# One two-bank PSUM tile and one maximum for the two score maps of a differential attention head

## The chip, the cores and the metric

The kernel runs on one core of a Trainium2 chip. The metric is the device time of one execution in microseconds (us). A core has a matrix engine (TensorE, PE in the profile), a vector engine (VectorE, DVE), a scalar engine (ScalarE, ACT), GpSimd (POOL) and SyncE (SP), whose queue issues nearly all of the DMA transfers here. Each engine works through its own instructions in the order of the program and waits for the others by semaphores.

## What is computed

One inference step of a two-layer transformer over 128 context tokens and 256 latent tokens, in fp32. Layer 0 mixes by retention and by windowed attention, layer 1 by differential attention and a Fourier transform, and a SwiGLU block follows each. The change concerns the differential attention of layer 1, cut from the reference:

```python
dq = dq.reshape(B, T, H_DIFF, 2, HEAD_DIM)        # 6 heads, 2 maps each, 64 wide
dk = dk.reshape(B, T, H_DIFF, 2, HEAD_DIM)
...
s = jnp.einsum('bqhmd,bkhmd->bhmqk', qb, keys).astype(f32) * (HEAD_DIM ** -0.5)
p = jax.nn.softmax(s, axis=-1)
p = p[:, :, 0] - lam_full * p[:, :, 1]
return jnp.einsum('bhqk,bkhe->bqhe', p.astype(vals.dtype), vals)
```

Every head has two softmax maps, and the second, times a factor, is subtracted from the first before the values are applied.

## The kernel before

The 384 tokens are three blocks of 128 rows: block 0 is the context, blocks 1 and 2 are the latent. A block of context has 128 keys, a latent block 384 (256 latent, 128 cached). So there are 18 items (block, head), and each has two score maps of 128 x 128 or 128 x 384.

`mixer_cd` computes layer 1's mixer. It projects the tokens with five slabs of 512 weight columns (`in_block`, line 377, tiles `cd`; three fp32r matmuls per product, from a weight split into a rounded part `r_` and a rest `l_` by ScalarE and VectorE, lines 173 and 175), transposes queries and keys into `dqT` and `dkT`, and calls `scores(upto)` three times between the slabs, for two heads each time. `scores` takes the items in the order of the list `items` and keeps `sc1` up to two items ahead of `sc2`.

`sc1(b, h)` computes the two maps of an item. Map m has its 64 features on partitions 64m to 64m+63 of `dqT` and `dkT`, so the two matmuls (lines 1216 and 118, tiles `ds`) use different rows of the array. Each matmul of fp32 is two records in the trace. Each map has a one-bank PSUM tile of its own out of four (`Banks("pcd", S=4)`, line 1154). VectorE takes the maximum of each map (line 1217, tile `dnm`), scales both by -0.125 (line 1219), and ScalarE forms the exponentials with their row sums (line 1223, tiles `dp` and `dsum`).

`sc2(b, h)` inverts the sums (line 1232), scales the second map (1233), adds it to the first (1234), and TensorE transposes the result in blocks of 128 x 128 (tiles `td`), which ScalarE copies (line 386). Between them TensorE has the projections `cd`, transpositions `tcd` of queries and keys, and the two Fourier steps `y` and `z`.

The order of the instructions on each engine is not written out. A scheduler lays them out when the program is built: work issued under `boost` (lines 116 to 121; among it the score matmuls, through `hmm`, and the transpositions) goes ahead of other work as soon as the scheduler holds it ready, and the projections fill in. On the chip each engine then keeps that fixed order.

The windowed attention of layer 0 (`win1`) also has two maps for each of its items and puts them in one tile of two banks (`bk.pair`, tiles `ws`), with one maximum (line 872, tile `wnm`).

Of the kernel before, what the change touches and what calls it, by code (L numbers as in the profile page):

```python
# [14 lines left out]
AF = mybir.ActivationFunctionType  # L15
ALU = mybir.AluOpType
AX = mybir.AxisListType
PSUM = bass.MemoryType.PSUM

P = 128  # L20
# [44 lines left out]
def trunk_kernel(ctx: ExitStack, tc: tile.TileContext, a: dict):  # L65
    nc = tc.nc
    mm = nc.tensor.matmul
    V, S, G, SY = nc.vector, nc.scalar, nc.gpsimd, nc.sync
# [4 lines left out]
    def opened(name, **kw):  # L73
        st = ExitStack()
        return st.enter_context(pool(name, **kw)), st
# [6 lines left out]
    def bankA(name):  # L82
        return psA.tile([P, 512], F32, tag="A", name=name)
# [19 lines left out]
    def small(shape, name):  # L103
        tick[0] += 1
        n = 1
        for s in shape[1:]:
            n *= s
        return perm.tile(shape, F32, tag=f"sm{n}", name=f"{name}{tick[0]}", bufs=SMALL[n])
# [4 lines left out]
    def mid(shape, name):  # L113
        return perm.tile(shape, F32, tag="uf", name=name, bufs=3)

    def boost(f, *args, **kw):
        with tc.high_priority(offset=BOOST):
            return f(*args, **kw)  # L118

    def hmm(*args, **kw):  # L120
        return boost(mm, *args, **kw)
# [1028 lines left out]
    def mixer_cd(u, cat, pto, u1, t1):  # L1150
        o_k = a["o_diff_k"][0, 0].rearrange("t h m d -> t (h m d)")
        o_v = a["o_diff_v"][0, 0].rearrange("t h d -> t (h d)")
        slab = cd_slab
        bk = Banks("pcd", S=4)
        ap, ap_es = opened("attn_cd")
        rope_of[0] = ap.tile([P, 2, 2, 64], F32, name="rope1")
        S.dma_start(rope_of[0], a["k_rope"].rearrange("b p s d -> p b s d"))
        if True:
            nlam, sub = lamd["nlam"], lamd["sub"]
            dqT = ap.tile([P, H_DIFF, NTOK], F32, name="dqT")  # L1160
            dkT = ap.tile([P, H_DIFF, 512], F32, name="dkT")
# [4 lines left out]
            for i, n in ((0, 4), (4, 2)):  # L1166
                t = mid([P, 512], f"ck{i}")
# [38 lines left out]
            def sc1(b, h):  # L1206
                nk = 1 if b == 0 else 3
                k0 = 0 if b == 0 else P
                w = nk * P
                nm = small([P, 2], "dnm")  # L1210
                sums = small([P, 2], "dsum")
                pss = []
                for m in range(2):
                    rows = slice(64 * m, 64 * m + 64)
                    ps = bk("S", f"ds{b}_{h}_{m}")
                    hmm(ps[:, 0:w], dqT[rows, h, b * P : (b + 1) * P], dkT[rows, h, k0 : k0 + w], start=True, stop=True)
                    V.reduce_max(nm[:, m : m + 1], ps[:, 0:w], AX.X)
                    pss.append(ps)
                V.tensor_scalar(nm, nm, -0.125, None, ALU.mult)
                pm = []  # L1220
                for m in range(2):
                    t = ap.tile([P, 384], F32, tag="p", name=f"dp{b}_{h}_{m}", bufs=5)
                    S.activation(t[:, 0:w], pss[m][:, 0:w], AF.Exp, bias=nm[:, m : m + 1], scale=0.125,
                                 accum_out=sums[:, m : m + 1])
                    pm.append(t)
                st_of[b, h] = (pm, sums)
# [18 lines left out]
            def scores(upto):  # L1245
                while state["n2"] < upto:
                    while state["n1"] < min(state["n2"] + 2, len(items)) and (state["n1"] < upto or upto == len(items)):
                        sc1(*items[state["n1"]])
                        state["n1"] += 1
                    sc2(*items[state["n2"]])  # L1250
                    state["n2"] += 1
# [59 lines left out]
            for b in range(NB):  # L1311
                ps = bankA(f"cd4_{b}")
# [6 lines left out]
            for b in range(NB):  # L1319
                ps = bankA(f"cd3_{b}")  # L1320
# [23 lines left out]
    m = {}  # L1344
    xscr = dram.tile([NB, P, D], F32, tag="xscr", name="xscr")
    for l in range(2):
# [9 lines left out]
        if l == 0:  # L1356
            def mod_ab(v, bk):
                mp = mod_pe(0, v, bk("M", f"mod0_{v}"))
                if v == 2:
                    m[0, v] = mod_scratch(mp, f"0_{v}")  # L1360
                else:
                    m[0, v] = mod_cols(mp, 0, v, bk("M", f"modt0_{v}"))

            pre, wxr_es = mixer_ab(u, cat, early, early_es, ap1, ap1_es, pto, *first, [lambda bk, v=v: mod_ab(v, bk) for v in (2, 3, 4)])
        else:
            cat, cat_es = open_cat(1)
            mixer_cd(u, cat, pto, m["s1"], m["t1"])
            pre, wxr_es = [], None
# [154 lines left out]
```

## Time and profile before

| | us |
|---|---|
| three timed runs | 1017.32, 1020.04, 1021.83 |
| their median | 1020.04 |
| the profiled execution | 1018.55 |
| its span, first to last instruction | 1016.8 |
| TensorE busy in it | 996.9 |
| VectorE busy | 637.9 |
| ScalarE busy | 432.9 |

The span is what the trace covers; the execution's own time is 1.75 us more. Busy time counts a matmul from its start to its modelled end, and matmuls are pipelined: a projection row lasts 0.40 us and the next one starts 0.23 us after it. Rows of one kind that follow each other directly are merged, with their count behind an x. What a matmul costs is therefore read from the start of one row to the start of the next. Time in brackets at the end of a row is idle time of the engine ahead of it, with what ended it.

### The profile page before, as it was taken

To read this page: it belongs to the slowest core of one execution; us is meant where nothing else is said; L and a number is where in the kernel's file an instruction comes from. 1 tells how busy PE (TensorE), PEld (TensorE's weight loads), DVE (VectorE), ACT (ScalarE), POOL (GpSimd) and SP (SyncE) were. 2 spreads that over 40 slices of the span, in tenths; PEclk is the share of its full clock that TensorE was granted. 3 is DMA by queue.
4 is the path that set the end of the run, shared out by engine and by line. 5 is a ranking of instruction groups with operands and counts; after the bars stand their busy time and mean duration, and the time that the engine had idled before them with its cause. 6 is when DMAs were issued, how large, how long until landed. Compare 5 with 4: busy or idle time off the path is not lost.

```text
span 1016.8 us, 14891 instructions
## 1 busy us (share of the span) xinstructions
PE 996.9 (98%) x5679; PEld 829.7 (82%) x5679; DVE 637.9 (63%) x1356; ACT 432.9 (43%) x786; POOL 1.2 (0%) x5
## 2 busy tenths in 40 slices
PE   9999999999999999999999999999999999999996
PEld 4775567688898988989987766787889999999985
DVE  5477558588785977968567677558843333335554
ACT  3385533227543333333428555544833333333410
POOL 0000000000000000000000000000000000000000
PEclk9999999999999999999999999999999999999998
DMA  9975446472896767676615322235574444444401
GB/s 305 294 203 187 146 132 205 171 254 94 281 301 219 217 211 253 208 235 208 207 63 161 95 88 93 83 103 224 184 252 146 125 125 124 125 125 127 161 22 41
DMA packets 109703, 172.85 MB, mean 170 GB/s; under 512 B 10176, under 2 KB 78272, under 8 KB 109632
## 3 DMA queue, kind: packets, MB, share of 16 engines
q1 hardware_dynamic: 106960, 170.87, 52.8%
q10 hardware_dynamic: 2672, 1.04, 0.4%
q8 instruction: 44, 0.72, 0.3%
q14 instruction: 27, 0.22, 0.1%
HBM read 167.52 MB, written 4.36 MB: 169 GB/s over the span
## 4 chain that ended last, share of the span: by engine, by line
PE 91%; DMA 3%; DVE 3%; ACT 2%; issue 1%; ACTq 0%; DVEq 0%
PE dn L518 17%; PE wu L542 17%; PE wg L542 17%; PE cd L377 8%; PE wo L377 6%; PE rvg L377 3%; PE s L377 3%; PE rqk L377 2%; DMA rawm<-in_w_mod 2%; PE ds L118 2%; PE hg L377 2%; PE mod L118 1%; PE hu L377 1%; PE ms L118 1%; PE po L118 1%; PE wpo L118 1%
## 5 line engine op out<-in xcount | busy, mean ns | idle before, releaser
L542 PE MATMUL wg<-ulf,r_wg 128*128 128x384 f32 x320 | 108.4, 339 | 0.0
L542 PE MATMUL wu<-ulf,r_wu 128*128 128x384 f32 x320 | 108.3, 338 | 0.0
L542 PE MATMUL wu<-urf,r_wu 128*128 128x384 f32 x320 | 108.2, 339 | 0.0
L542 PE MATMUL wg<-urf,l_wg 128*128 128x384 f32 x320 | 108.1, 338 | 0.0
L542 PE MATMUL wu<-urf,l_wu 128*128 128x384 f32 x320 | 108.1, 338 | 0.0
L542 PE MATMUL wg<-urf,r_wg 128*128 128x384 f32 x320 | 108.0, 339 | 0.0
L175 DVE TENSOR_TENSOR l_wg<-raw_wg,r_wg 128x1024 fp32r<-128x1024 f32 x40 | 48.7, 1223 | 68.4 <-ACT r_wg L173 68.4
L249 DVE SCALAR_TENSOR_TENSOR z<-mraw,cs,z 128x1024 f32<-128x1024 f32 x70 | 86.3, 1280 | 8.3 <-DMA mraw<-in_w_mod 8.0
L175 DVE TENSOR_TENSOR l_wd<-raw_wd,r_wd 128x1024 fp32r<-128x1024 f32 x36 | 44.0, 1223 | 53.7 <-ACT r_wd L173 53.7
L173 ACT CAST r_wd<-raw_wd 128x1024 fp32r<-128x1024 f32 x36 | 37.8, 1050 | 87.0 <-PE wu L542 40.1
L175 DVE TENSOR_TENSOR l_wu<-raw_wu,r_wu 128x1024 fp32r<-128x1024 f32 x40 | 48.6, 1222 | 40.1 <-ACT r_wu L173 40.1
L173 ACT CAST r_wg<-raw_wg 128x1024 fp32r<-128x1024 f32 x40 | 42.0, 1050 | 73.0 <-PE dn L518 29.9
L173 ACT CAST r_wu<-raw_wu 128x1024 fp32r<-128x1024 f32 x40 | 42.0, 1049 | 64.6 <-issue 24.2
L518 PE MATMUL dn<-l_wd,hr 128*128 128x512 f32 x168 | 66.6, 396 | 0.0
L518 PE MATMUL dn<-r_wd,hr 128*128 128x512 f32 x168 | 66.5, 396 | 0.0
L518 PE MATMUL dn<-r_wd,hl 128*128 128x512 f32 x168 | 66.5, 396 | 0.0
L542 PEld LDWEIGHTS wg<-urf,r_wg 128*128 128x128 f32 x320 | 60.1, 188 | 1.9 <-issue 0.8
L542 PEld LDWEIGHTS wu<-urf,r_wu 128*128 128x128 f32 x320 | 60.1, 188 | 1.7 <-ACT r_wg L173 0.8
L542 PEld LDWEIGHTS wu<-ulf,r_wu 128*128 128x128 f32 x320 | 60.1, 188 | 0.5
L542 PEld LDWEIGHTS wg<-ulf,r_wg 128*128 128x128 f32 x320 | 60.1, 188 | 0.5
L542 PEld LDWEIGHTS wg<-urf,l_wg 128*128 128x128 f32 x320 | 60.1, 188 | 0.0
L542 PEld LDWEIGHTS wu<-urf,l_wu 128*128 128x128 f32 x320 | 60.1, 188 | 0.0
(418 smaller groups left out, 2180.0 us busy)
## 6 DMA issues: line engine op xcount, KB each, us to landing
raw_wd<-in_w_down SPq DMA_DIRECT2D x44, 512.0 KB
rawm<-in_w_mod SPq DMA_DIRECT2D x40, 512.0 KB
mraw<-in_w_mod SPq DMA_DIRECT2D x40, 512.0 KB
raw_wg<-in_w_gate SPq DMA_DIRECT2D x40, 512.0 KB
raw_wu<-in_w_up SPq DMA_DIRECT2D x40, 512.0 KB
raw_cd<-in_w_in_cd SPq DMA_DIRECT2D x20, 512.0 KB
ms<-in_w_mod SPq DMA_DIRECT2D x16, 512.0 KB
raw_rqk<-in_w_in_ab SPq DMA_DIRECT2D x16, 256.0 KB
```

What stands on the lines that cost most here:

```text
L118: return f(*args, **kw)
L173: S.copy(r, t)
L175: V.tensor_tensor(lo, t, r, ALU.subtract)
L249: V.scalar_tensor_tensor(z[c], t, cs[:, c, k : k + 1], z[c], ALU.mult, ALU.add)
L377: op = mm(ps[:, col : col + width], u[pu][:, k0 + kk, b * P : (b + 1) * P], (r, lo)[pw][:, kk, :], start=(first and i == 0 and pu + pw == ...
L518: mm(acc[b, nh], h[fc][ph][:, b * P : (b + 1) * P], wrl[pw][:, nh * 512 : (nh + 1) * 512], start=(fc == 0 and ph + pw == 0), stop=(last an ...
L542: mm(ps[j][:, 0:NTOK], un[i][pw][:, k, j * P : (j + 1) * P], u2[pu][:, 4 * i + k, :], start=(i == 0 and k == 0 and pu + pw == 0), stop=(i ...
```

## The change

The two maps of an item share one tile of two banks: `bk.pair` gives a tile of 2 x 512 columns, of which there are two (S=2, the same four banks). Map m is written to bank m of it. One `reduce_max` over both banks writes both maxima, after the loop instead of in it. Scale, exponentials and everything behind them are as before.

```diff
-        bk = Banks("pcd", S=4)
+        bk = Banks("pcd", S=2)
...
-                pss = []
+                ps = bk.pair("S", f"ds{b}_{h}")
                 for m in range(2):
                     rows = slice(64 * m, 64 * m + 64)
-                    ps = bk("S", f"ds{b}_{h}_{m}")
-                    hmm(ps[:, 0:w], dqT[rows, h, b * P : (b + 1) * P], dkT[rows, h, k0 : k0 + w], start=True, stop=True)
-                    V.reduce_max(nm[:, m : m + 1], ps[:, 0:w], AX.X)
-                    pss.append(ps)
+                    hmm(ps[:, m, 0:w], dqT[rows, h, b * P : (b + 1) * P], dkT[rows, h, k0 : k0 + w], start=True, stop=True)
+                V.reduce_max(nm, ps[:, :, 0:w], AX.X)
                 V.tensor_scalar(nm, nm, -0.125, None, ALU.mult)
...
-                    S.activation(t[:, 0:w], pss[m][:, 0:w], AF.Exp, bias=nm[:, m : m + 1], scale=0.125,
+                    S.activation(t[:, 0:w], ps[:, m, 0:w], AF.Exp, bias=nm[:, m : m + 1], scale=0.125,
```

Two lines fewer in the file move the lines behind: the maximum is line 1216 in the new file, its scaling 1217, the reciprocal 1230, the scaling of the second map 1231, the subtraction 1232.

Since the scheduler lays out the order from the instructions and their tiles, it is another one around the scores. On TensorE, in head 1, the old order has, from the first map of block 1 on (ds1_1_0 is block 1, head 1, map 0; the last number of a name is only a counter):

```order
L118 MATMUL ds1_1_0_5932<-dkT_5470,dqT_5469 128x384
L118 MATMUL ds1_1_1_5935<-dkT_5470,dqT_5469 128x384
L118 MATMUL tcd2_0_5810<-ident_69,t1cd2_0_5776 128x128 x4
L118 MATMUL ds2_1_0_5952<-dkT_5470,dqT_5469 128x384
L118 MATMUL td2_0_5925<-ident_69,dp2_0_0_5895 128x128 x3
L118 MATMUL ds2_1_1_5955<-dkT_5470,dqT_5469 128x384
L377 MATMUL cd2_1_5779<-r_cd2_0_5590,ul1_5057 128x512
L118 MATMUL td0_1_5947<-ident_69,dp0_1_0_5917 128x128
L377 MATMUL cd2_1_5779<-l_cd2_0_5591,ur1_5056 128x512
L118 MATMUL ds0_2_0_6094<-dkT_5470,dqT_5469 128x128
```

and the new one, from the transposition tcd2_0 on:

```order
L118 MATMUL tcd2_0_5810<-ident_69,t1cd2_0_5776 128x128 x4
L377 MATMUL cd2_1_5779<-l_cd2_0_5591,ur1_5056 128x512
L118 MATMUL ds1_1_5924<-dkT_5470,dqT_5469 128x384 x2
L118 MATMUL td2_0_5917<-ident_69,dp2_0_0_5889 128x128 x3
L118 MATMUL ds2_1_5942<-dkT_5470,dqT_5469 128x384 x2
L118 MATMUL td0_1_5937<-ident_69,dp0_1_0_5909 128x128
L377 MATMUL cd2_1_5779<-r_cd2_1_5596,ur1_5056 128x512
L377 MATMUL cd2_1_5779<-r_cd2_1_5596,ul1_5057 128x512
L377 MATMUL cd2_1_5779<-l_cd2_1_5597,ur1_5056 128x512
L377 MATMUL cd2_1_5779<-r_cd2_1_5596,ur1_5056 128x512
L118 MATMUL ds0_2_6082<-dkT_5470,dqT_5469 128x128 x2
```

Both maps of an item stand together in the new order (x2), and what stood between them stands before or behind. On TensorE in head 3, the old order reads, from block 1 on:

```order
L118 MATMUL ds1_3_0_6171<-dkT_5470,dqT_5469 128x384
L118 MATMUL td1_2_6142<-ident_69,dp1_2_0_6114 128x128 x3
L118 MATMUL ds1_3_1_6174<-dkT_5470,dqT_5469 128x384
L118 MATMUL ds2_3_0_6191<-dkT_5470,dqT_5469 128x384
L118 MATMUL td2_2_6164<-ident_69,dp2_2_0_6134 128x128 x3
L118 MATMUL ds2_3_1_6194<-dkT_5470,dqT_5469 128x384
L118 MATMUL z0_0_6438<-y0_0_6433,cpe_6300 128x128
L118 MATMUL td0_3_6186<-ident_69,dp0_3_0_6156 128x128
```

and the new one:

```order
L118 MATMUL ds1_3_6151<-dkT_5470,dqT_5469 128x384 x2
L118 MATMUL td2_2_6144<-ident_69,dp2_2_0_6116 128x128 x3
L118 MATMUL ds2_3_6169<-dkT_5470,dqT_5469 128x384 x2
L118 MATMUL td0_3_6164<-ident_69,dp0_3_0_6136 128x128
L118 MATMUL z0_0_6402<-y0_0_6397,cpe_6276 128x128 x2
```

The transposition td0_3 now stands right behind the pair ds2_3, ahead of the Fourier step z. On VectorE at the same place the old order is:

```order
L1217 TENSOR_REDUCE dnm144_6169<-ds1_3_1_6174 128x1
L1232 RECIPROCAL dsum143_6148<-dsum143_6148 128x2
L1219 TENSOR_SCALAR dnm144_6169<-dnm144_6169 128x2
L1233 TENSOR_SCALAR dp0_3_1_6158<-dp0_3_1_6158,dsum143_6148,nlam_759 128x128
L1234 SCALAR_TENSOR_TENSOR dp0_3_0_6156<-dp0_3_0_6156,dsum143_6148,dp0_3_1_6158 128x128
L1217 TENSOR_REDUCE dnm146_6189<-ds2_3_0_6191 128x1
```

and the new one:

```order
L1232 SCALAR_TENSOR_TENSOR dp2_2_0_6116<-dp2_2_0_6116,dsum141_6110,dp2_2_1_6118 128x384
L1230 RECIPROCAL dsum143_6130<-dsum143_6130 128x2
L1231 TENSOR_SCALAR dp0_3_1_6138<-dp0_3_1_6138,dsum143_6130,nlam_759 128x128
L1216 TENSOR_REDUCE dnm144_6149<-ds1_3_6151 128x2
L1232 SCALAR_TENSOR_TENSOR dp0_3_0_6136<-dp0_3_0_6136,dsum143_6130,dp0_3_1_6138 128x128
```

The joint maximum of ds1_3 stands between the scaling of dp0_3_1 and the subtraction into dp0_3_0, which td0_3 reads. On ScalarE only neighbouring instructions change places around the scores; the queue of SyncE with the DMA issues and GpSimd are as before.

## Rows read from the trace of the kernel before

**Rows 1.** The page, busy time, share of the span, instructions: TensorE

```profile
PE 996.9 (98%) x5679; PEld 829.7 (82%) x5679; DVE 637.9 (63%) x1356; ACT 432.9 (43%) x786; POOL 1.2 (0%) x5
```

**Rows 2.** Busy time by windows (from:to, length, engines, clock, DMA share, GB/s)

```profile
591.02:605.70 14.68, 14.58 (x65) 8.72 (x64) 9.60 (x31) 8.84 (x29) 0.00 (x0) 1.00 0.15 52
617.51:646.90 29.39, 28.45 (x127) 16.70 (x126) 21.98 (x68) 19.26 (x65) 0.00 (x0) 1.00 0.06 22
```

**Rows 3.** Waits of the DMA queue, 560 to 720: total, times, longest

```profile
SPq L164 <- DVE l_cd L175: 78.4, 15, 32.3
```

**Rows 4.** Timeline of TensorE, windowed attention, one item: start, duration, instruction

```profile
104.19 0.92 PE L118 MATMUL ws<-wkT,wqT 64*128 64x384 f32 x4
105.04 0.28 PE L118 MATMUL ws<-wmb,identb 128*128 128x128 bf16 x2
```

**Rows 5.** Timeline of TensorE, heads 1 and 2 of the differential attention

```profile
594.41 1.47 PE L118 MATMUL ds<-dkT,dqT 64*128 64x384 f32 x4
595.81 0.66 PE L118 MATMUL tcd<-ident,t1cd 128*128 128x128 f32 x4
...
597.71 0.91 PE L118 MATMUL ds<-dkT,dqT 64*128 64x384 f32 x2
598.55 0.50 PE L377 MATMUL cd<-r_cd,ul 128*128 128x512 f32 x1
...
600.08 0.39 PE L377 MATMUL cd<-r_cd,ul 128*128 128x512 f32 x1
600.39 0.48 PE L118 MATMUL ds<-dkT,dqT 64*128 64x128 f32 x2
600.81 0.50 PE L377 MATMUL cd<-l_cd,ur 128*128 128x512 f32 x1
601.14 0.39 PE L377 MATMUL cd<-r_cd,ur 128*128 128x512 f32 x1
601.37 0.40 PE L377 MATMUL cd<-r_cd,ul 128*128 128x512 f32 x1
```

**Rows 6.** Timeline of TensorE, heads 3 to 5

```profile
620.77 0.49 PE L118 MATMUL ds<-dkT,dqT 64*128 64x128 f32 x2 [0.70 <-ACT dp L1223]
...
634.84 0.30 PE L118 MATMUL td<-ident,dp 128*128 128x128 f32 x1 [0.16 <-DVE dp L1234]
...
636.83 0.91 PE L118 MATMUL ds<-dkT,dqT 64*128 64x384 f32 x2
637.67 0.55 PE L118 MATMUL td<-ident,dp 128*128 128x128 f32 x3
638.15 1.91 PE L118 MATMUL ds<-dkT,dqT 64*128 64x384 f32 x6
639.99 0.55 PE L118 MATMUL td<-ident,dp 128*128 128x128 f32 x3
```

**Rows 7.** Instructions by tile, ds and ws: shortest/median/longest ns, first and last start, forms

```profile
L1217 DVE TENSOR_REDUCE dnm<-ds x36: 279/549/558, 575.0 to 640.8; 128x1 f32<-128x384 f32 x24, 128x1 f32<-128x128 f32 x12
L1223 ACT ACTIVATE dp<-ds,dnm x36: 357/580/609, 575.7 to 642.3; 128x384 f32<-128x384 f32 x24, 128x128 f32<-128x128 f32 x12
...
L872 DVE TENSOR_REDUCE wnm<-ws x12: 412/954/958, 66.3 to 129.2; 128x2 f32<-128x768 f32 x8, 128x2 f32<-128x256 f32 x4
```

**Rows 8.** Timeline of VectorE, heads 2 to 4

```profile
619.84 0.17 DVE L1219 TENSOR_SCALAR dnm<-dnm 128x2 f32<-128x2 f32 x1
619.92 1.02 DVE L1217 TENSOR_REDUCE dnm<-ds 128x1 f32<-128x384 f32 x2
...
626.46 0.35 DVE L1234 SCALAR_TENSOR_TENSOR dp<-dp,dsum,dp 128x128 f32<-128x128 f32 x1
...
634.35 0.34 DVE L1234 SCALAR_TENSOR_TENSOR dp<-dp,dsum,dp 128x128 f32<-128x128 f32 x1
```

## The prediction

> **What bounds the kernel now.** The page comes first. TensorE is busy for 996.9 of 1016.8 us [rows 1], but its matmuls are pipelined and a busy row may hide a wait, so the starts of successive rows have to be read, not the busy share. The change touches the scores of the differential attention alone. In the order of TensorE's instructions the two programs differ in two stretches: 591.02 to 605.70 us (heads 0 to 2) and 617.51 to 646.90 us (heads 2 to 5). The view by windows gives both [rows 2]: TensorE is busy 14.58 of 14.68 and 28.45 of 29.39 us, VectorE only 9.60 and 21.98, the clock is granted in full (1.00, the upper level), and DMA moves little (0.15 and 0.06 of its share). So TensorE's own queue sets the pace here. What is saved on TensorE in these 44 us should come off the end: behind them the weight loads wait for buffers that VectorE's splits free (78.4 us in 15 waits [rows 3]), these splits wait for matmuls, and so loads start earlier with TensorE.
>
> **What is removed: maps that ran alone.** The two maps of a head use rows 0 to 63 and 64 to 127 of the array. The windowed attention at the start already has its two maps in one two-bank tile, which is the nearest row for the new form. Side by side, its two maps (four records) start at 104.19, and the next instruction starts at 105.04: 0.85 us for both [rows 4]. One map alone, two records, costs as much: 597.71 to 598.55, 0.84 us [rows 5]. Two maps next to each other overlap; two with something between them cost double.
>
> I counted, in the old order, the maps that have something else between them. Of 384 columns: in heads 1 and 4 one pair stands apart. In heads 3 and 5 two pairs do, but the second map of one stands beside the first of the next, so three slots serve where two would. In head 5: 0.84 from 636.83 to 637.67, then 1.84 from 638.15 to 639.99 [rows 6], which is 0.85 + 0.84 with a wait of 0.15. That is one slot of 0.84 us too many in each of four heads: **3.4 us**. Of 128 columns: in heads 2 to 5 block 0's maps stand apart. A map alone between full matmuls costs 600.08 to 600.39, to 600.81, to 601.14 [rows 5], that is 0.31 + 0.42 + 0.33 less two full matmuls of 0.23 (601.14 to 601.37): 0.60 us. Three heads save this; in head 5 the second map stands among other short work and saves its 0.42. Together **2.2 us**. In the new order both maps of every pair are adjacent, so all of it goes.
>
> Old waits go too. The pair at 594.41 takes 1.40 us to 595.81 instead of 0.85, since its second map waits for a bank: 0.55 us [rows 5]. Before 620.77 TensorE is idle for 0.70, for an exponential; before 634.84 for 0.16 [rows 6]; with the 0.15 of head 5 that is 1.0 us. **Removed: 3.4 + 2.2 + 0.55 + 1.0 = 7.15 us of TensorE's time.**
>
> **What is shortened beside TensorE.** 36 maxima become 18. Two separate ones of 384 columns take 2 x 549 ns, and the joint one of 768 takes 954 ns in the windowed attention [rows 7]: 144 ns saved, twelve times. Two of 128 columns take 2 x 279, joint 412: 146 ns, six times. The sum, 2.6 us of VectorE, I cost at nothing by itself: VectorE idles 7.4 us of the second stretch [rows 2]. It acts only where TensorE waits for VectorE, and there it is in the walk below. The exponentials stay 36.
>
> **What is added: new waits.** Two of them. First, a slot is now two banks: a pair waits until *both* exponentials of the pair two before are done, where its first map waited for the first alone; one exponential of 384 columns is 580 ns [rows 7]. Behind the waiting pair stand the whole of TensorE's in-order queue, the long projections among it. Second, on VectorE the joint maximum cannot start before both maps are done, and the scheduler has put it ahead of work that TensorE needs. In head 3 the old order ran the subtraction of dp0_3 right behind its scaling; in the new order the maximum of ds1_3 stands between them, and the transposition td0_3 waits for that subtraction.
>
> I walked the new order through with the rows' durations, each instruction as early as its engine's queue, its row's duration and what it waits for allow. At this place, from the start of pair ds1_3: its end is at 0.92 [rows 4]; behind it the three transpositions of td2_2 (0.48, as 637.67 to 638.15 [rows 6]) and the pair ds2_3 let td0_3 come up at 2.27. On VectorE the subtraction of dp2_2, the reciprocal and the scaling are done at 1.50. The maximum then takes 0.95 [rows 7] and the subtraction 0.35 (626.46 [rows 8]). It starts some 0.08 before the maximum ends, as the maximum at 619.92 starts 0.09 before the scaling of 619.84 ends [rows 8]: 2.72. From VectorE to TensorE it is another 0.15 (634.35 + 0.34 [rows 8], then 634.84 [rows 6]): 2.87: a wait of 0.60 us. The other waits over 0.2 us in this walk are td0_1 0.33, the pair ds0_3 0.32 (second exponential), td2_3 0.27, td0_4 0.46, td0_5 0.33 and td1_5 0.21. **Added: 2.5 us.** Smaller gaps stand in both orders and are left out on both sides. No row shows these waits, so both ends: nothing, if the maxima come earlier than I have them; at most all of what is removed and more, if each of the twelve pairs in the tight parts waits as long as the worst wait shown, 0.70: 8.4 us. I take 2.5, which is nearest to what the old order has in the same places (1.0 + 0.55).
>
> VectorE's load in the second stretch is 21.98 us of 29.39 [rows 2]; TensorE's part would shrink to about 24 without new waits, so VectorE fits, but with little room. On this the Trainium skill warns ("TensorEngine Tiling (Array Packing)", Performance Considerations, PSUM Bottleneck): tiling makes TensorE faster but not the emptying of PSUM, which may become the bottleneck. By that rule the gain would stop where VectorE is full; by the row it isn't full yet, and the rule's case is the second rival below.
>
> **The sum.** 7.15 - 2.5 = 4.65 us less. The profiled execution took 1018.55 us (span 1016.8 and 1.75 around it); 4.65 less is 1013.9. The median of the three timed runs is 1020.04, which would give 1015.4. The median of all four times shown is 1019.3, and from it I forecast **1014.7 us**. About 0.5% (5.1 us) is what a measurement of this kernel can tell from no change, so the forecast lies just inside of it.
>
> **Rivals.** *The new waits don't come.* Then 7.15 us go: 1012.2. For it: VectorE idles in both stretches, and the joint maximum is shorter. Against it: the subtraction stands behind the maximum in a fixed order. *VectorE's chain becomes the bound.* Each of twelve pairs in the tight parts waits some 0.4 us for maximum, subtraction and transposition, the middle of what the walk found: 4.8 us given back, 2.35 gained, 1016.9. For it: VectorE is busy three quarters of the second stretch already. Against it: only seven places in the walk waited as long as 0.2. *The slots bind, slower than before.* With two slots of two banks every pair waits one exponential longer than a first map did: 12 x 0.58 = 7.0 us, on top of the 2.5: 9.5 given back against 7.15, 1021.6. It decides from 0.6 us a pair. The Trainium skill points that way ("Perfetto Trace Analysis", Optimizing Tensor Performance, Matmuls): independent groups should rotate through different banks, so that emptying one overlaps the next group's matmuls. No row of the new form shows such a wait, and between pairs the new order has transpositions and projections, which cover most of it. *That the change does not do what it says* can be left out: in the new order the two matmuls of each pair stand together, and the windowed attention shows that two maps in one tile overlap [rows 4].
>
> **Chances.** Forecast (3.2 to 6.0 us gained) 0.60; no new waits (over 6.0) 0.16; VectorE's chain (0 to 3.2) 0.19; slots (slower) 0.05. Of the forecast's 0.60 some 0.22 lies over 5.1 us, so faster by over 0.5% 0.22 + 0.16 = 0.38, within 0.5% 0.38 + 0.19 = 0.57, slower 0.05. Low end: all of 7.15 and 0.7 for the spread of the runs, 1011.5. High end: 1 us gained, 1018.3, which leaves out the slower case and a part of the third.
>
> **What would show it.** In the profile of after: every pair's four records in one row of 0.85 us, and no two-record rows; these two stretches shorter by 2 and 3 us; the wait of td0_3 for the subtraction at about 0.6 us, those of score pairs for exponentials at 0.3 or less; 18 maxima at 954 and 412 ns; and all behind it shifted by the same amount. The forecast is wrong if TensorE's idle time before score pairs passes 3 us, if a pair stays at 1.7 us, or if the weight loads behind don't move with TensorE.

## The result

| | us, median (lowest to highest) |
|---|---|
| before, 4 runs | 1019.37 (1017.32 to 1021.83) |
| after, 4 runs | 1012.06 (1011.55 to 1012.68) |
| ratio | 0.9929, 95% interval 0.9909 to 0.9948 |
| profiled execution, before and after | 1018.55 and 1011.62 |
| its span, before and after | 1016.8 and 1009.8 |

The changed kernel is faster by 0.7%, more than the 0.5% that can be told from no change. 1014.7 had been forecast, and the time lies in the range, at its lower part. A second measurement of the same kernel gave less, 0.56% (first experiment below). Of the kernel of e4 and e8 one execution each is left out, at 1043.12 and 1042.73 us (mean granted clock 0.979, 0.995 or more in all others); that of e4 was its profiled one, with the clock at its lower level from 635.9 to 670.0 us, so the kernel ran once more for a profile (e8).

**Where the time went.** Every profile has a row by which the program can be cut into three: the first score row (tile `ds`), the row of 36 matmuls `dpv` at the end of the attention, and the end. Timeline of TensorE after (start, duration, instruction, count; idle time before it in brackets):

```profile
572.96 0.49 PE L118 MATMUL ds<-dkT,dqT 64*128 64x128 f32 x4
...
667.90 4.19 PE L118 MATMUL dpv<-dv,dpT 128*128 128x128 f32 x36
```

In the profile of before the same rows start at 574.49 and 674.47. So, in us:

| | before | after | difference |
|---|---|---|---|
| start to the first score row | 574.49 | 572.96 | -1.53 |
| first score row to the `dpv` row | 99.98 | 94.94 | -5.04 |
| `dpv` row to the end | 342.28 | 341.92 | -0.36 |

The middle part holds all that the change touches. The two stretches in which the orders differ, by windows (from:to, length, then busy time of PE, PEld, DVE, ACT and POOL with their instructions, granted clock, DMA share, GB/s), each from the same instruction to the same as in [rows 2]:

```profile
589.52:602.41 12.89, 12.47 (x66) 7.66 (x64) 9.05 (x26) 8.58 (x28) 0.00 (x0) 1.00 0.18 59
614.30:640.27 25.97, 24.11 (x127) 14.66 (x126) 21.22 (x58) 18.75 (x64) 0.00 (x0) 1.00 0.05 20
```

12.89 instead of 14.68 and 25.97 instead of 29.39 [rows 2]: 1.79 + 3.42 = 5.21 us less, where 4.65 had been forecast. (0.17 of it goes back in small gaps between and around them.) TensorE's busy time fell by 6.8 us, from 996.9 [rows 1], with the same number of instructions:

```profile
PE 990.1 (98%) x5679; PEld 826.9 (82%) x5679; DVE 636.3 (63%) x1338; ACT 432.4 (43%) x786; POOL 1.2 (0%) x5
```

**The pairs.** Heads 1 and 2 on TensorE, the place of [rows 5]:

```profile
594.31 0.92 PE L118 MATMUL ds<-dkT,dqT 64*128 64x384 f32 x4
595.34 0.52 PE L118 MATMUL td<-ident,dp 128*128 128x128 f32 x3
595.79 0.92 PE L118 MATMUL ds<-dkT,dqT 64*128 64x384 f32 x4
596.99 0.30 PE L118 MATMUL td<-ident,dp 128*128 128x128 f32 x1 [0.28 <-DVE dnm L1217]
...
598.24 0.49 PE L118 MATMUL ds<-dkT,dqT 64*128 64x128 f32 x4
598.66 0.50 PE L377 MATMUL cd<-r_cd,ul 128*128 128x512 f32 x1
```

Every row of scores has four records or eight (two pairs); the rows of two records of [rows 5] and [rows 6] are gone. A pair of 384 columns lasts 0.92 in its row, as in [rows 4], and one of 128 columns takes 0.42 us from its start to the next start (598.24 to 598.66), as much as a single map of 128 took in [rows 5].

Rows beside score maps change their cost too. In before the four transpositions `tcd` at 595.81 [rows 5] stand between score maps, in after between projections (the row behind them in before, then both rows in after):

```profile
596.40 0.91 PE L118 MATMUL ds<-dkT,dqT 64*128 64x384 f32 x2
```

```profile
593.55 0.60 PE L118 MATMUL tcd<-ident,t1cd 128*128 128x128 f32 x4
593.90 0.47 PE L377 MATMUL cd<-l_cd,ur 128*128 128x512 f32 x1
```

From start to start the transpositions take 0.59 us there and 0.35 here.

**The new waits.** Heads 3 to 5, the place of [rows 6]:

```profile
614.62 1.56 PE L118 MATMUL ds<-dkT,dqT 64*128 64x384 f32 x8
616.11 0.50 PE L377 MATMUL cd<-r_cd,ul 128*128 128x512 f32 x1
...
618.13 0.49 PE L118 MATMUL ds<-dkT,dqT 64*128 64x128 f32 x4 [0.36 <-ACT dp L1221]
...
621.71 0.92 PE L118 MATMUL ds<-dkT,dqT 64*128 64x384 f32 x4
623.13 0.30 PE L118 MATMUL td<-ident,dp 128*128 128x128 f32 x1 [0.50 <-DVE dnm L1217]
...
627.49 0.52 PE L118 MATMUL td<-ident,dp 128*128 128x128 f32 x3 [0.21 <-DVE dp L1232]
...
629.50 0.30 PE L118 MATMUL td<-ident,dp 128*128 128x128 f32 x1 [0.23 <-DVE dp L1232]
...
635.07 0.30 PE L118 MATMUL td<-ident,dp 128*128 128x128 f32 x1 [0.22 <-DVE dnm L1217]
...
637.31 0.40 PE L377 MATMUL cd<-r_cd,ur 128*128 128x512 f32 x1
637.85 0.52 PE L118 MATMUL td<-ident,dp 128*128 128x128 f32 x3
```

The brackets are the idle time before a row. The wait of 0.50 is that of td0_3. Its releaser is named by the maximum's scaling (line 1217), which ends next to the subtraction that td0_3 reads; the queue of VectorE shows what stands in the way:

```profile
621.51 0.35 DVE L1231 TENSOR_SCALAR dp<-dp,dsum,nlam 128x128 f32<-128x128 f32 x1
621.77 0.95 DVE L1216 TENSOR_REDUCE dnm<-ds 128x2 f32<-128x768 f32 x1
622.64 0.34 DVE L1232 SCALAR_TENSOR_TENSOR dp<-dp,dsum,dp 128x128 f32<-128x128 f32 x1
```

The scaling, then the joint maximum with its 0.95 us, then the subtraction: it ends at 622.98, and td0_3 starts 0.15 later, as predicted. Added up by line, 560 to 690 us (engine, line, released by; total, times, longest):

```profile
PE td L118 <- DVE dnm L1217: 1.0, 3, 0.5
PE td L118 <- DVE dp L1232: 0.4, 2, 0.2
PE ds L118 <- ACT dp L1221: 0.4, 1, 0.4
```

With the 0.30 us before 637.85 (0.54 from start to start instead of the 0.24 between projections) these seven waits are 2.1 us. A bracket counts from the modelled end of the row ahead, which lies behind the point at which the next row could have started: the pair at 621.71 takes 0.84 us to the next start, so td0_3 comes 0.58 late (623.13 - 621.71 - 0.84) where its bracket has 0.50. From start to start, as the prediction's walk counts, the seven are 2.6 us. The maxima by tile:

```profile
L1216 DVE TENSOR_REDUCE dnm<-ds x18: 416/949/957, 573.5 to 634.9; 128x2 f32<-128x768 f32 x12, 128x2 f32<-128x256 f32 x6
```

18 of them, at the durations that the windowed attention had shown [rows 7]. And the weight loads moved with TensorE: their waits for the splits fell by 4.5 us from 78.4 [rows 3]:

```profile
SPq L164 <- DVE l_cd L175: 73.9, 15, 28.6
```

### The profile page after: what moved, and what is told of

Read it like the earlier page. It is cut to its first block, busy times and chain, and to the rows that moved or that the text cites. A ratio compares the mean times of both kernels' runs of the same rounds, so it can differ in the third digit from the quotient of the medians.

```text
span 1009.8 us, 14877 instructions
## 1 busy us (share of the span) xinstructions
PE 990.1 (98%) x5679; PEld 826.9 (82%) x5679; DVE 636.3 (63%) x1338; ACT 432.4 (43%) x786; POOL 1.2 (0%) x5
## 4 chain that ended last, share of the span: by engine, by line
PE 87%; DVE 5%; DMA 3%; ACT 3%; issue 1%; SPq 0%; ACTq 0%; DVEq 0%
PE dn L518 17%; PE wg L542 17%; PE wu L542 16%; PE cd L377 7%; PE wo L377 5%; PE rvg L377 4%; PE s L377 2%; PE rqk L377 2%; PE hg L377 2%; PE mod L118 2%; PE hu L377 1%; DMA rawm<-in_w_mod 1%; PE ms L118 1%; PE wpo L118 1%; PE ws L118 1%
```

## The experiments

The theory (A): two maps that stand next to each other on TensorE overlap, two that are apart cost double, and the gain is what TensorE's own queue saves by that, less the new waits. Its rivals: the joint maximum gives the gain; VectorE's chain sets the pace; the slots bind; the gain is chance ahead of the scores. The middle part, from the first score row to the `dpv` row, is given for each profile, since it repeats from one execution to the next within 0.03 us.

### e1: the changed kernel once more

No edit.

> The changed kernel, unedited, a second time. Theory A (the gain is made in the two score stretches alone: 1.8 us in the first and 3.4 in the second by the two traces, and the 1.5 us that the changed kernel was ahead before its first score row is chance): the first score row starts anywhere within 2 us of 574, the stretches are again 12.9 and 26.0 us, and the gain over the kernel before is 4.5 to 6 us, ratio 0.994 to 0.9955. Theory B (the change also gains 1.5 us ahead of the scores every time): the first score row starts again at 573.0 or earlier, and the gain is again about 7 us, ratio 0.993.

Measured: 1013.57 us (1013.31 to 1014.01, 5 runs) against 1019.34, ratio 0.9944 (0.9932 to 0.9955). The two stretches by windows:

```profile
591.18:604.07 12.89, 12.48 (x65) 7.66 (x64) 9.07 (x26) 8.57 (x28) 0.00 (x0) 1.00 0.17 60
615.98:641.91 25.93, 24.10 (x128) 14.65 (x126) 21.22 (x58) 18.70 (x64) 0.00 (x0) 1.00 0.05 20
```

They are as long as in the first profile of after. But the first score row starts at 574.64, where before had it at 574.49: the 1.53 us ahead of the scores in the first comparison aren't there. The middle part is 94.91 us, against 94.94.

### e7: the kernel before once more

No edit.

> The kernel before, unedited, for a second profile. If the 1.5 us by which the changed kernel's first profile was ahead before the first score row was chance of that execution, the first score row of this one may stand anywhere from 572.5 to 575.5 us, and from the first of the two stretches on the lengths are as in the first profile: 14.7 and 29.4 us, each within 0.2. If it belonged to the change, the first score row stands at 574.5 again.

Measured: 1019.42 us (1017.61 to 1022.68, 8 runs), ratio 1.0004 (0.9983 to 1.0025). The first score row and the stretches:

```profile
575.64 0.49 PE L118 MATMUL ds<-dkT,dqT 64*128 64x128 f32 x4
```

```profile
592.17:606.85 14.68, 14.59 (x65) 8.72 (x64) 9.60 (x31) 8.87 (x29) 0.00 (x0) 1.00 0.15 52
618.70:648.08 29.38, 28.42 (x127) 16.71 (x126) 21.99 (x68) 19.29 (x65) 0.00 (x0) 1.00 0.05 17
```

Lengths as in [rows 2] within 0.01 us, the middle part 100.01 against 99.98, while the first score row came 1.15 us later than in the first profile. Over all profiles compared here it starts anywhere from 572.96 to 575.78, although TensorE's order is the same in all of them ahead of it. So 5.0 to 5.1 us belong to the change, and what lies ahead of the scores or behind the attention scatters from profile to profile.

### e2: one tile, two maxima

The pair's tile as in the change, but one maximum for each bank:

```diff
-                V.reduce_max(nm, ps[:, :, 0:w], AX.X)
+                for m in range(2):
+                    V.reduce_max(nm[:, m : m + 1], ps[:, m, 0:w], AX.X)
```

> The shared two-bank tile stays, the joint maximum is split into two again, one for each bank. Theory A (the gain comes from the two maps standing side by side on TensorE): nearly as fast as the changed kernel, 0.3 to 1.5 us slower, since two maxima take 1.02 us where one takes 0.95, and one of the 18 pairs is apart in this program's order. Theory B (the single maximum makes the gain, VectorE being what TensorE waits for): most of the gain is lost, within 2 us of the kernel before.

Measured: 1013.1 us (1012.26 to 1018.67, 9 runs), ratio 0.9958 (0.9941 to 0.9976), beside 1013.57 for the changed kernel on the same chip: by the times no slower, where 0.3 to 1.5 us had been expected. By tile, and the waits:

```profile
L1217 DVE TENSOR_REDUCE dnm<-ds x36: 270/548/558, 574.9 to 638.5; 128x1 f32<-128x384 f32 x24, 128x1 f32<-128x128 f32 x12
```

```profile
PE td L118 <- DVE dsum L1231: 0.5, 1, 0.5
PE ds L118 <- ACT dp L1222: 0.4, 1, 0.4
PE td L118 <- DVE dp L1233: 0.3, 1, 0.3
...
PE td L118 <- DVE dnm L1218: 0.2, 1, 0.2
```

The 36 maxima are back, the gain stays. The middle part is 95.38 us, 0.44 longer, and one pair of 384 columns stands apart in this order. Without the joint maximum the waits for line 1218 shrink, and others of about the same sum take their place. So the joint maximum by itself gives nothing that can be told from the scatter.

### e3 and e4: a small matmul behind the pair, or between its maps

A matmul of 8 columns over all 128 rows, whose result nobody reads, added to each pair. In e3 it follows the second map, directly in all but three places (two of the eighteen pairs come apart in the order); in e4 it stands between the maps (all come apart). e3:

```diff
-                    hmm(ps[:, m, 0:w], dqT[rows, h, b * P : (b + 1) * P], dkT[rows, h, k0 : k0 + w], start=True, stop=True)
+                    with (tc.issue_after(last_mm.ins) if m == 1 else nullcontext()):
+                        last_mm = hmm(ps[:, m, 0:w], dqT[rows, h, b * P : (b + 1) * P], dkT[rows, h, k0 : k0 + w], start=True, stop=True)
+                    if m == 1:
+                        with tc.issue_after(last_mm.ins):
+                            hmm(ps[:, 0, 384:392], ident, ident[:, 0:8], start=True, stop=True)
```

and e4:

```diff
+                    if m == 1:
+                        with tc.issue_after(last_mm.ins):
+                            last_mm = hmm(ps[:, 0, 384:392], ident, ident[:, 0:8], start=True, stop=True)
-                    hmm(ps[:, m, 0:w], dqT[rows, h, b * P : (b + 1) * P], dkT[rows, h, k0 : k0 + w], start=True, stop=True)
+                    with (tc.issue_after(last_mm.ins) if m == 1 else nullcontext()):
+                        last_mm = hmm(ps[:, m, 0:w], dqT[rows, h, b * P : (b + 1) * P], dkT[rows, h, k0 : k0 + w], start=True, stop=True)
```

> The changed kernel with one more matmul of 8 columns over all 128 rows, of no use, right behind each pair of score maps: 18 of them. Its two maps stay side by side but for two of the eighteen pairs in this program's order. It is the control for the next one. Both theories: 18 times 0.1 to 0.2 us and two pairs apart at 0.84 each, 3 to 5 us slower than the changed kernel, about 1016.

> The same small matmul, between the two maps of each pair instead of behind them: all 18 pairs are apart, tile, slots and maximum are as in the changed kernel. Theory A (side by side, two maps cost what one does): ten pairs of 384 columns more than in the control at 0.84 us and six of 128 at 0.42, 10 to 12 us slower than the control, about 1027. Theory B (what counts is the slots and the maximum, not the neighbourhood): within 2 us of the control.

Measured: e3 1015.62 us (1015.39 to 1017.02, 4 runs), ratio 0.9966 (0.9952 to 0.9979). e4 1025.03, 1026.78 and 1027.5, ratio 1.0069 (1.0052 to 1.0086). The same instructions, with the small one moved by one place, cost 11.2 us (1026.8 - 1015.6) and turn the gain into a loss. Against e1, e3 is 2.05 us slower, where 3 to 5 had been expected; its middle part is 99.05 us, 4.1 longer than after's. Its rows of head 0, block 2:

```profile
591.09 0.92 PE L118 MATMUL ds<-dkT,dqT 64*128 64x384 f32 x4
591.93 0.39 PE L118 MATMUL ds<-ident 128*128 128x8 f32 x2
592.18 0.42 PE L118 MATMUL td<-ident,dp 128*128 128x128 f32 x2
```

The pair and the small matmul take 1.09 us, 0.84 + 0.25.

### e8: between, for a profile

The kernel of e4.

> The kernel of the run before with the small matmul between the two maps, once more, for a profile that can be compared. Theory A (maps apart cost double): all eighteen pairs as two rows of two records with the small matmul between them; a map of 384 columns alone takes 0.84 us from its start to the next start, so that a pair takes about 1.9 us with the small matmul where it takes 0.85 + 0.25 with the small matmul behind; from the first score row to the end 450 to 452 us, against 439.9 us with the small matmul behind. Rival (the small matmul itself disturbs, by waits for banks or exponentials): pairs under 1.4 us, and the difference stands as idle time in brackets ahead of score rows.

Measured: 1028.72 and 1026.37 us, ratio 1.0081 (1.0046 to 1.0116). The same place as the last rows of e3:

```profile
594.60 0.91 PE L118 MATMUL ds<-dkT,dqT 64*128 64x384 f32 x2
595.44 0.39 PE L118 MATMUL ds<-ident 128*128 128x8 f32 x2
595.75 0.91 PE L118 MATMUL ds<-dkT,dqT 64*128 64x384 f32 x2
596.60 0.44 PE L118 MATMUL td<-ident,dp 128*128 128x128 f32 x2
...
598.11 0.79 PE L377 MATMUL cd<-r_cd,ur 128*128 128x512 f32 x1
598.70 0.63 PE L377 MATMUL cd<-r_cd,ul 128*128 128x512 f32 x1
```

From the first score row to the end this profile has 451.16 us, and e3's has 439.97, as expected. 0.84 + 0.31 + 0.85 = 2.00 us for the pair where e3 has 1.09: the second map costs 0.91 by being apart, and no idle time stands before any of these rows. Since the wait inside the row at 594.41 [rows 5] has no bracket either, the starts are the better sign: 0.84 and 0.32 return at the pair of 632.19, 633.03 and 633.35, so it isn't a wait for a bank or an exponential. For pairs of 128 columns the same comparison gives 1.15 against 0.67, so 0.48. The middle part is 109.92 us, 10.87 longer than e3's. Ten pairs at 0.91 and six at 0.48 are 12.0; in two places the second map stands beside the first of the next pair (rows of four at 626.24 and 650.28), which saves some 0.8 each; and e3's waits for VectorE, 0.8, are absent. That leaves 9.6. The rest is clock: the last two rows above last longer than the 0.40 of a projection, and by windows

```profile
598.00:602.00 4.00, 4.00 (x14) 3.06 (x12) 1.54 (x5) 2.07 (x7) 0.00 (x0) 0.57 0.19 66
```

the granted clock is 0.57 there, between its two levels (0.50, 1.2 GHz, and 1.00, 2.4 GHz) and mostly at the lower. Eight projections take 3.52 us (598.11 to 601.63), where e3 has 1.94 (593.19 to 595.13): 1.6 us. 9.6 + 1.6 = 11.2, against 10.87 measured.

### e5: one slot instead of two

```diff
-        bk = Banks("pcd", S=2)
+        bk = Banks("pcd", S=1)
```

> The changed kernel with one two-bank slot for score pairs instead of two, so that each pair's matmuls wait until both exponentials of the pair directly before are done (in the changed kernel: of the pair two before). In the order all eighteen pairs keep their two maps together, and TensorE gets more projections between one pair and the next, so that transpositions of the maps come later. Theory A (the slots are covered by other work): at most 2 us slower than the changed kernel, 1012 to 1015 us, no wait of a score pair over 0.5 us. Rival (slots bind): behind each pair 0.92 + 0.95 + 0.17 + 2 x 0.58 = 3.2 us pass before the next may start; twelve pairs in tight parts, of which projections fill two thirds, give 12 us more, 1024 to 1026 us, and the waits stand ahead of score rows, ended by exponentials.

Measured: 1012.94 us (1011.42 to 1015.52, 8 runs), ratio 0.9932 (0.9911 to 0.9952), no slower than with two slots. The middle part is 94.03 us, 0.9 shorter than after's. Three pairs in a row, and the largest wait of the attention, 560 to 690 us:

```profile
592.78 0.92 PE L118 MATMUL ds<-dkT,dqT 64*128 64x384 f32 x4
...
596.57 0.49 PE L118 MATMUL ds<-dkT,dqT 64*128 64x128 f32 x4
...
599.39 0.92 PE L118 MATMUL ds<-dkT,dqT 64*128 64x384 f32 x4
```

```profile
PE td L118 <- DVE dp L1232: 1.2, 3, 0.5
```

No score pair waits for an exponential at all. The scheduler spreads the pairs, 2.8 to 3.8 us apart here where after's start 1.2 to 3.2 us apart at the same place (589.95, 591.16, 594.31, 595.79), and fills with projections; the last pair starts at 655.48 instead of 633.94. The slots don't bind: half of them serve as well, in this kernel, as long as projections are left to fill in. In its one profile the 0.9 us come back behind the `dpv` row (342.7 us to the end instead of 341.9), so no gain is claimed.

### e6: each maximum twice

```diff
                 V.reduce_max(nm, ps[:, :, 0:w], AX.X)
+                V.reduce_max(nm, ps[:, :, 0:w], AX.X)
```

> The changed kernel with every joint maximum taken twice in a row into the same numbers: VectorE gets 12 x 0.95 + 6 x 0.41 = 13.9 us more in these stretches. In the order two of the eighteen pairs come apart (1.7 us). Theory A (VectorE has room; TensorE's own queue is the bound): the two pairs and some 2 us of new waits, 3 to 5 us slower than the changed kernel, 1016 to 1018 us. Rival (VectorE's chain already sets the pace behind the pairs): most of the 13.9 us comes through, 10 us or more, over 1022 us.

Measured: 1014.11 us (1012.06 to 1016.95, 10 runs), ratio 0.995 (0.9934 to 0.9966): slower than the changed kernel by 0.5 (against e1) to 2.1 us (against the first measurement), less than even the theory had expected. The middle part is 95.79 us, 0.85 longer, although VectorE is busy 11.2 us longer in it (72.78 against 61.61) and two pairs come apart. VectorE has room for that in this order, which also spreads the pairs: the last starts 70.9 us behind the first score row, where after has 61.0. In after's own order the doubled maxima were not tried. This profile is of the slowest of the ten executions, and it shows a reason behind the attention (waits, then two windows):

```profile
PE dot L118 <- DVE catl L392: 1.7, 1, 1.7
```

```profile
676.00:678.00 2.00, 0.29 (x2) 0.00 (x0) 0.74 (x2) 1.94 (x7) 0.00 (x0) 1.00 0.00 0
...
680.00:682.00 2.00, 2.00 (x12) 2.00 (x11) 1.40 (x9) 0.00 (x0) 0.00 (x0) 0.50 0.66 133
```

In the other order a transposition waits 1.7 us instead of 0.2 at about 676 to 678, and from 680 to 682 TensorE has the lower clock level. Whether the faster executions have it too isn't shown.

## Why the prediction was right where it was, and where not

- **What bounds the kernel.** Right. TensorE's queue was said to set the pace, with VectorE beside it. e6 makes VectorE busy for 11.2 us more and costs the attention 0.85; e4 puts nothing more than e3 on any engine, moves one instruction of each pair, and costs 11.2 (in e8's profile some 1.6 of it is clock).
- **Removed, 7.15 us.** The terms named came, but the sum is 0.65 too small: the stretches lost 5.21 net of 2.6 us of new waits, so 7.8 gross. Added up from each start to the next, the score rows of 384 columns lost 4.0 us besides the new waits, where 3.4 + 0.55 + 0.15 = 4.1 had been counted. So what is missing lies with the maps of 128 columns and with the rows beside score maps, whose own cost the prediction took as unchanged. The transpositions `tcd` alone make 0.24 of it (under "The pairs"); the rest was not traced to single rows. The price of a map apart, 0.84 and 0.42 to 0.60, was measured by itself at 0.91 and 0.48 (e8 against e3).
- **The joint maximum at nothing.** Right: with 36 maxima the time is the same (e2). The 2.6 us of VectorE was too much, since it took two single maxima at 2 x 549 ns where [rows 8] have two in a row in 1.02 us; VectorE's busy time fell by 1.6 us (637.9 to 636.3).
- **New waits, 2.5 us.** Right within 0.1. All seven places came. From start to start: td0_3 0.58 (0.60 predicted), td0_4 0.37 (0.46), td0_1 0.36 (0.33), td0_5 0.29 (0.33), ds0_3 0.43 (0.32), td2_3 0.28 (0.27), td1_5 0.30 (0.21), together 2.6. Two gaps that the walk had left out as small are about 0.2 each (ahead of 595.34 and 621.26). The score pair's wait for an exponential was to be 0.3 or less; its bracket has 0.36.
- **The sum, 4.65 us.** The change is worth 5.0 to 5.1 (100.0 to 94.9 in two profiles each), so the forecast was 0.4 short; by 5.0 the time would be 1014.3. The first measurement has 7.3 us less. In its profile 5.04 of 6.93 are in the attention, 1.53 ahead of the first score row, where the profiles compared here scatter by 2.8 us, and 0.36 behind. So the distance from 1014.7 to 1012.06 is a small miss of a term and a larger part outside of what the change touches. That part is not only chance of single executions: the first measurement's four lie between 1011.55 and 1012.68 us, e1's five between 1013.31 and 1014.01. What sets the two occasions apart isn't shown.
- **The rival without new waits** gave 1012.2, nearest to the first measurement, and was still wrong: the waits are there. A time alone would have confirmed the wrong story.
- **VectorE's chain (1016.9) and the slots (1021.6).** Both fell. Each pair would have had to wait 0.4 or 0.6 us; after has one pair that waits for an exponential, 0.36. e5 took away half of the slots and e6 doubled VectorE's maxima, each in an order that spreads the pairs more, and neither came near these times. The Trainium skill's PSUM Bottleneck ("TensorEngine Tiling (Array Packing)", Performance Considerations) isn't reached here: VectorE is busy 21.22 of 25.97 us in the second stretch, and doubling its maxima cost little. The Trainium skill names it there for a fourfold speedup of TensorE. The Trainium skill's advice to rotate independent groups through banks ("Perfetto Trace Analysis", Optimizing Tensor Performance, Matmuls) speaks against one slot more than against two; the runs show one slot no slower, because other matmuls overlap with the emptying instead.

## What to carry to other kernels

Two matmuls that use different rows of the array are worth what their neighbours in the queue make of them: give both one tile, so that the scheduler holds them ready together (in e2, e3 and e6 one or two pairs still came apart), and look in the order whether anything of all 128 rows stands between them. Whether holding the two maps together in tiles of their own would do as well was not tried. Count such places before and after and price them from a row of the same kernel that already has the good form; here that gave 7.15 us where 7.8 were measured. And cut a profile at rows that both kernels have: the cut part repeated within 0.03 us, while whole executions scatter by several.

## What the runs showed that was not expected

- A second pair directly behind a pair costs less than the first: two take 1.49 us (614.62 to 616.11 in after), not 2 x 0.85.
- A map alone costs as much as two side by side, also with only a matmul of 8 columns between them (0.84 and 0.85 in e8, 0.84 for the pair in e3).
- Apart from the last 7 us of every span, the granted clock fell in two of the profiles compared, each time at one place. In e8 to 0.57 over 598 to 602 us, after 3.5 us of work (594.60 to 598.11) in which only single maps, small matmuls and two transpositions ran and no row was idle. In e6 to 0.50 over 680 to 682 us, after the window 676 to 678 in which TensorE was busy 0.29 of 2.00 us. The maps apart in the kernel before did not do it: its clock is 1.00 in both stretches [rows 2].
- Half of the PSUM banks for the scores served as well as all four (e5), which leaves two banks for something else.
